# Another order of the column-group products, and two more load buffers beside the scatters, in an S5 + attention + expert block

## The chip, the cores and the metric

The kernel runs on one core of a Trainium2 chip. The core has a tensor engine (PE, which loads its weights as PEld), a vector engine (DVE), a scalar engine (ACT), GpSimd (POOL) and a sync engine (SP) that here issues nearly all loads. Sixteen DMA engines move data between HBM and the on-chip memory. The metric is the device time of one execution in microseconds (us); less is better.

## What is computed

One block over 256 tokens of width 2048, in fp32: a state-space mixer (S5) and a sparse attention side by side, a gated sum into the stream, and then a layer of 16384 experts of which each token uses 128. Cut to what the change touches:

```python
cond = jax.nn.silu(c) @ w_ada[l] + b_ada[l]                      # six vectors of 2048
sh1, sc1, g1, sh2, sc2, g2 = [m[:, None, :] for m in jnp.split(cond, N_ADA, axis=-1)]
...
y = (jnp.einsum('ghp,blgp->blgh', c_re, sr) - jnp.einsum('ghp,blgp->blgh', c_im, si)
     + d_skip * uf)                                              # S5's output from its states
...
x = x + g2 * peer(h2, w_q, k1, k2, exp_u, exp_v)
...
# peer: top 16 of 256 candidates in each of 8 heads -> expert ids ec, gates gc
a = jax.nn.gelu(jnp.einsum('cd,chkd->chk', xc, exp_u[ec]))
return jnp.einsum('chk,chkd->cd', gc * a, exp_v[ec])
```

## The kernel before

**Arithmetic.** A product of two fp32 matrices is made of three products of rounded halves. split() makes them from a loaded unit of 128 x 1024: ACT casts to hi (L99), DVE subtracts to lo (L102). lin_block() (L521) then runs hi*hi, hi*lo and lo*hi.

**Loads.** unit() (L91) lets SP issue a load of 512 KB into a ring called raw, of four buffers. SP's queue is in order: a load that waits for its buffer holds those behind it. w_ada goes through rings of its own, in the later stages through adap alone, with three buffers.

**Order.** The Tile framework's scheduler, with its own simulation of the times, sets the order of the instructions on each engine. What the program writes in a loop may therefore be taken apart and stand elsewhere on the engine, as early as its operands are expected.

**cond_job() (L440)** multiplies silu(c) by w_ada. A step takes two loads, which hold four tiles of 512 columns: tiles[0] and [1] are of the first load, [2] and [3] of the second. Four products follow (L449), each into 32 rows of one PSUM tile, so each uses another group of 32 columns of PE. There are 80 such steps of four, called quads here, spread over the first 620 us beside the other work.

**g2_job() (L1314)** does the same with one row of output for g2: two loads of w_g2 through raw, four products (L1318), 16 steps. It runs beside the g groups and the expert tiles from 884 to 1310 us. g2_end() (L1322) adds b_row to the four rows and stores them.

**s5_py() (L691)** takes the four results p, q, a2, c2 that DVE makes in that order (L683 to L686), and adds their products with CP into one PSUM tile (L710), in the order of the list quad["pq", n] (L687).

**u_tile() (L1151)** handles 128 experts of exp_u: two loads, two splits, 48 products into pa, and a gelu (L1165), which is multiplied into SA or SB. There are 128 of them, from 620 to 1573 us.

**Scatters.** look() finds the tokens of each expert tile, and places() (L1355 to L1396, scratch in a pool st) turns this into a place for each row, by products psx and a chain on DVE. After places(0, ...) the pool st is closed, and a pool gq takes memory there; before the change it holds the small tile of g2_end alone. The loop at L1428 runs one u_tile and four scatters (L1414, POOL's indirect DMAs from SA to wc) in turn, 88 scatters in all. Behind it, from 1573 to the end, the rows of exp_v are gathered and multiplied.

## Time and profile before

| | us |
|---|---|
| median of three runs | 1891.27 |
| the runs | 1888.39 to 1891.78 |
| the profiled execution | 1887.95 |
| its span | 1886.1 |
| PE busy in it | 1781.8 |
| DVE busy | 1381.6 |
| ACT busy | 804.6 |
| POOL busy | 824.4 |

The stages, in us from the start of the span: to 49 start and first parts of w_ada; to 188 the first input products and more of w_ada; to 377 S5 steps beside w_in; to 620 attention, its output and w_out; to 884 the queries and the top-k of the experts, beside expert tiles; to 1310 the g groups beside expert tiles and w_g2; to 1400 expert tiles and places(); to 1573 scatters beside the last expert tiles; to 1886 the rows of exp_v.

The profile is of one execution. A line of a timeline gives the start, the length, the engine, the line of the program, and what the instruction writes and reads; idle time before it stands in brackets with what ended it. A product L449 or L1318 of fp32 operands is two instructions in the trace, so four instructions there are two products here. Lengths of products overlap; the distance from one start to the next is what a product holds PE for.

### The profile page before, as it was taken

How to read it: one execution, taken by the hardware profiler on the slowest of the kernel's cores; microseconds unless marked ns; L12 is line 12 of the kernel's file. 1: busy time of each engine (PE TensorE's matmuls, PEld its weight loads, DVE VectorE, ACT ScalarE, POOL GpSimd, SP SyncE). 2: the span in 40 equal slices, each digit the busy share in tenths (PEclk: the TensorE clock that was granted, in tenths of full speed). 3: DMA queues.
4: the chain of work that ended last, by engine and by line, in shares of the span. 5: the costliest groups of instructions: out<-in, count | busy, mean ns of one | idle time of the engine just before them, and what ended most of it. 6: DMA issues, size and time to landing. Idle time of an engine off the chain costs nothing. (4 is left out here: it accounts for less than half of the span.)

```text
span 1886.1 us, 32604 instructions
## 1 busy us (share of the span) xinstructions
PE 1781.8 (94%) x12048; PEld 1488.0 (79%) x12048; DVE 1381.6 (73%) x2765; ACT 804.6 (43%) x1329; POOL 824.4 (44%) x926
## 2 busy tenths in 40 slices
PE   5999999999999899999999999999998999999895
PEld 2756655568666899999999898898998898777674
DVE  3636998756745698888999898998783457776666
ACT  3422211148634544444444444444432336555554
POOL 5923432201110210112787666665027665887532
PEclk9998999999999999999999999999998999999998
DMA  9987556785686455555565556556567779999972
GB/s 358 407 286 265 192 185 226 260 314 199 238 268 208 166 180 179 171 178 167 184 194 193 190 183 196 184 178 201 182 186 218 227 233 356 323 326 323 373 258 109
DMA packets 117839, 436.77 MB, mean 232 GB/s; under 512 B 17237, under 2 KB 19989, under 8 KB 107686
## 3 DMA queue, kind: packets, MB, share of 16 engines
q1 hardware_dynamic: 91440, 322.41, 51.3%
q0 software_dynamic: 22080, 108.62, 16.2%
q10 hardware_dynamic: 4150, 3.56, 0.6%
q8 instruction: 97, 1.59, 0.3%
q14 instruction: 72, 0.59, 0.1%
HBM read 411.38 MB, written 23.15 MB: 230 GB/s over the span
## 5 line engine op out<-in xcount | busy, mean ns | idle before, releaser
L102 DVE TENSOR_TENSOR lo<-raw,hi 128x1024 fp32r<-128x1024 f32 x382 | 512.9, 1345 | 229.6 <-ACT hi L99 188.3
L99 ACT CAST hi<-raw 128x1024 fp32r<-128x1024 f32 x385 | 402.1, 1047 | 590.7 <-PE pa L521 302.2
L521 PE MATMUL pa<-hhi,lo 128*128 128x256 f32 x2048 | 590.3, 288 | 10.1 <-DVE lo L102 6.7
L521 PE MATMUL pa<-hhi,hi 128*128 128x256 f32 x2048 | 583.6, 285 | 9.7 <-ACT hi L99 6.8
L521 PE MATMUL pa<-hlo,hi 128*128 128x256 f32 x2048 | 583.1, 285 | 0.0
L521 PEld LDWEIGHTS pa<-hhi,lo 128*128 128x128 f32 x2048 | 395.0, 193 | 38.3 <-DVE lo L102 11.1
L521 PEld LDWEIGHTS pa<-hhi,hi 128*128 128x128 f32 x2048 | 395.3, 193 | 10.8 <-ACT hi L99 8.0
L521 PEld LDWEIGHTS pa<-hlo,hi 128*128 128x128 f32 x2048 | 395.3, 193 | 0.5 <-issue 0.5
L1287 POOL TENSOR_TENSOR mv<-o,gp 128x256 fp32r<-128x256 f32 x256 | 186.4, 748 | 124.9 <-DVE o L1284 65.8
L1505 DVE TENSOR_TENSOR lv<-rv,hv 128x1024 fp32r<-128x1024 f32 x144 | 173.1, 1229 | 55.7 <-ACT hv L1504 52.3
L1504 ACT CAST hv<-rv 128x1024 fp32r<-128x1024 f32 x144 | 146.3, 1049 | 63.6 <-DMA rv<-in_peer_v,wt 40.7
L1284 DVE TENSOR_TENSOR o<-pT,iota 128x256 fp32r<-128x256 f32 (+1 forms) x256 | 124.8, 502 | 30.8 <-PE pgs L1290 17.9
L449 PE MATMUL cps<-adap,scz 128*32 128x512 f32 x476 | 113.8, 622 | 16.4 <-DMA adap<-in_w_ada 16.4
L1205 POOL TENSOR_TENSOR eq<-eq,iff 128x512 f32<-128x512 f32 x16 | 30.0, 1896 | 212.1 <-DVE eq L1204 212.1
L1305 POOL TENSOR_TENSOR SA<-SA,gs 128x50 f32<-128x50 f32 (+42 forms) x128 | 113.8, 904 | 12.9 <-ACT SA L1162 12.5
L1414 POOL DMA_INDIRECT wc<-SA,slot x88 | 97.1, 1103 | 46.1 <-issue 25.2
L1459 POOL DMA_INDIRECT rv<-in_peer_v,wt x74 | 97.3, 1316 | 45.2 <-DVE lv L1505 17.5
L521 PE MATMUL lin<-hhi,hi 128*128 128x256 f32 x352 | 104.8, 298 | 2.2 <-ACT sg L998 1.3
L521 PE MATMUL lin<-hlo,hi 128*128 128x256 f32 x352 | 102.9, 292 | 1.5 <-POOL hlo L1111 1.0
L521 PE MATMUL lin<-hhi,lo 128*128 128x256 f32 x352 | 102.6, 292 | 0.0
L1295 ACT COPY gs<-pgs 128x256 f32<-128x256 f32 x128 | 47.6, 373 | 121.7 <-POOL SA L1305 107.5
L521 PEld LDWEIGHTS lin<-hhi,hi 128*128 128x128 f32 x352 | 68.1, 194 | 26.3 <-issue 16.9
(450 smaller groups left out, 3291.9 us busy)
## 6 DMA issues: line engine op xcount, KB each, us to landing
raw<-in_peer_u SPq DMA_DIRECT2D x256, 512.0 KB
adap<-in_w_ada SPq DMA_DIRECT2D x119, 512.0 KB
raw<-in_w_in SPq DMA_DIRECT2D x32, 512.0 KB
raw<-in_w_out SPq DMA_DIRECT2D x32, 512.0 KB
raw<-in_peer_wq SPq DMA_DIRECT2D x32, 512.0 KB
raw<-in_w_g SPq DMA_DIRECT2D x32, 512.0 KB
raw<-in_w_inq SPq DMA_DIRECT2D x16, 512.0 KB
raw<-in_cmp_w SPq DMA_DIRECT2D x16, 512.0 KB
```

The source lines that it names most:

```text
L99: i = nc.scalar.copy(hi[:, :n], raw[:, :n])
L102: (lo_engine or nc.vector).tensor_tensor(out=lo[:, :n], in0=raw[:, :n], in1=hi[:, :n].bitcast(F32), op=OP.subtract)
L449: nc.tensor.matmul(ps[32 * g:32 * g + 32, :], scz[:, kt + g], tiles[g], start=kt == 0, stop=kt == KT - 4)
L521: nc.tensor.matmul(ps, w, a[:, kk], start=first and u == 0 and k == 0 and i == 0, stop=last and u == n - 1 and k == 7 and i == 2)
L1284: nc.vector.tensor_tensor(out=o, in0=bc(pT[:, j, t:t + 2].unsqueeze(2), shp), in1=io, op=OP.is_equal)
L1287: nc.gpsimd.tensor_tensor(out=mv[:, :, j], in0=o2, in1=g, op=OP.mult)
L1295: nc.scalar.copy(tmp, pv[:, 1])
L1305: nc.gpsimd.tensor_tensor(out=o, in0=o, in1=tmp[:, a0:m], op=OP.mult)
L1414: d = nc.gpsimd.indirect_dma_start(out=wcs[i], out_offset=bass.IndirectOffsetOnAxis(ap=ap, axis=0), in_=SB[:, m - NSA] if i else SA[:, m], ...
L1459: d = nc.gpsimd.indirect_dma_start(out=raw, out_offset=None, in_=A["peer_v"], in_offset=bass.IndirectOffsetOnAxis(ap=wt[:, 128:129].bitcas ...
L1504: nc.scalar.copy(hi, raw)
L1505: state["last"] = nc.vector.tensor_tensor(out=lo, in0=raw, in1=hi.bitcast(F32), op=OP.subtract).ins
```

## The change

Three things are altered. The loops over the column groups in cond_job and g2_job run 2, 3, 0, 1 and not 0 to 3, and the list of s5_py's operands begins with c2, which DVE makes last. g2_end puts its rows into a buffer of the ring raw. And gq now holds a ring rawx of two buffers, which u_tile uses for two of each six loads from the scatter loop to the end of the expert tiles: six buffers in all.

```diff
--- before.py
+++ after.py
@@ -445,7 +445,8 @@
             tiles = loaded[ran[0]]
             assert loads[ran[0]] == (j, q, kt // 2)
             ran[0] += 1
-            for g in range(4):
+
+            for g in (2, 3, 0, 1):
                 nc.tensor.matmul(ps[32 * g:32 * g + 32, :], scz[:, kt + g], tiles[g],
                                  start=kt == 0, stop=kt == KT - 4)
             if kt == KT - 4:
@@ -684,7 +685,7 @@
         v.tensor_tensor(out=q, in0=c, in1=ei, op=OP.mult)
         v.tensor_tensor(out=a2, in0=a, in1=ei, op=OP.mult)
         v.tensor_tensor(out=c2, in0=c, in1=er, op=OP.mult)
-        quad["pq", n] = (0, p), (2, q), (1, a2), (1, c2)
+        quad["pq", n] = (1, c2), (0, p), (2, q), (1, a2)
 
     zs = {"todo": [], "go": False}
 
@@ -1152,7 +1153,12 @@
         m = state["m"]
         if m >= NK:
             return
-        us = [split(unit(A["peer_u"][m, i]), keep=m == NK - 1) for i in range(2)]
+        us = []
+        for i in range(2):
+
+            more = state.get("more") and (2 * m + i) % 6 >= 4
+            r = unit(A["peer_u"][m, i], state["more"], "rawx", 2) if more else unit(A["peer_u"][m, i])
+            us.append(split(r, keep=m == NK - 1))
         ps = psA.tile([128, 512], F32, name="pa", tag="pa", bufs=2)
         lin_block(us, h2hi, h2lo, ps[:, :T])
         t = state["t"]
@@ -1314,13 +1320,13 @@
         for kt in range(KT):
             rs = [unit(A["w_g2"][kt * 128:(kt + 1) * 128, h * 1024:(h + 1) * 1024])
                   for h in range(2)]
-            for g in range(4):
+            for g in (2, 3, 0, 1):
                 nc.tensor.matmul(g2ps[32 * g:32 * g + 1, :], scol[:, kt:kt + 1],
                                  rs[g // 2][:, g % 2 * 512:(g % 2 + 1) * 512], start=kt == 0, stop=kt == KT - 1)
             yield
 
-    def g2_end(pool):
-        rows = pool.tile([128, 512], F32, name="g2r", tag="g2r")
+    def g2_end():
+        rows = buf("raw")[:, :512]
         for g in range(4):
             cs, r = slice(g * 512, (g + 1) * 512), slice(32 * g, 32 * g + 1)
             nc.gpsimd.dma_start(rows[r], A["b_row"][1:2, cs])
@@ -1427,7 +1433,8 @@
     sts.close()
     gqs = ExitStack()
     gq = gqs.enter_context(tc.tile_pool(name="gq", bufs=1))
-    g2_end(gq)
+    g2_end()
+    state["more"] = gq
     seen, sent = SORT, 0
     while sent < SORT:
         u_tile()
@@ -1478,6 +1485,7 @@
         if state["m"] >= seen + 8:
             look(seen, seen + 8)
             seen += 8
+    state["more"] = None
     gqs.close()
     psU.close()
```

On PE at the first row of w_g2 in the stage of the g groups (L1318 psg before; pa are expert tiles, pgs the g groups). Before:

```order
4158 L521 MATMUL pa<-hhi,lo 128x256
4159 L521 MATMUL pa<-hhi,hi 128x256
4160 L521 MATMUL pa<-hlo,hi 128x256
4161 L1318 MATMUL psg<-raw,scol 1x512 x2
4162 L521 MATMUL pa<-hhi,lo 128x256
...
4183 L1290 MATMUL pgs<-mv,o_8841 128x256 x2
4184 L521 MATMUL pa<-hhi,lo 128x256
4185 L521 MATMUL pa<-hhi,hi 128x256
4186 L521 MATMUL pa<-hlo,hi 128x256
4187 L1318 MATMUL psg<-raw,scol 1x512 x2
4188 L521 MATMUL pa<-hhi,lo 128x256
```

After the change, where the lines have moved down by six (L1318 is L1324, L521 is L522):

```order
4155 L522 MATMUL pa<-hhi,lo 128x256
4156 L522 MATMUL pa<-hhi,hi 128x256
4157 L522 MATMUL pa<-hlo,hi 128x256
4158 L1296 MATMUL pgs<-mv,o_8841 128x256 x2
4159 L1324 MATMUL psg<-raw,scol 1x512 x4
4160 L522 MATMUL pa<-hhi,lo 128x256
4161 L522 MATMUL pa<-hhi,hi 128x256
4162 L522 MATMUL pa<-hlo,hi 128x256
```

The two pairs, 26 rows apart before, are one run of four at the second one's place. The same holds for all 16 rows.

On PE near the end of w_out's products (L1013, lin), with the w_ada products of cond_job between them (L449, cps). Before:

```order
1979 L1013 MATMUL lin<-hi,mlo 128x512 x2
1980 L449 MATMUL cps<-adap,scz 32x512 x2
1981 L1013 MATMUL lin<-hi,mhi 128x512 x2
1982 L1013 MATMUL lin<-lo,mhi 128x512 x2
1983 L1013 MATMUL lin<-hi,mlo 128x512 x2
1984 L1013 MATMUL lin<-hi,mhi 128x512 x2
1985 L1013 MATMUL lin<-lo,mhi 128x512 x2
1986 L1013 MATMUL lin<-hi,mlo 128x512 x2
1987 L449 MATMUL cps<-adap,scz 32x512 x2
1988 L1013 MATMUL lin<-hi,mhi 128x512 x2
```

After (L1014 and L450):

```order
1994 L1014 MATMUL lin<-lo,mhi 128x512 x2
1995 L1014 MATMUL lin<-hi,mlo 128x512 x2
1996 L1014 MATMUL lin<-hi,mhi 128x512 x2
1997 L450 MATMUL cps<-adap,scz 32x512 x4
1998 L1014 MATMUL lin<-lo,mhi 128x512 x2
1999 L1014 MATMUL lin<-hi,mlo 128x512 x2
2000 L1014 MATMUL lin<-hi,mhi 128x512 x2
2001 L1014 MATMUL lin<-lo,mhi 128x512 x2
```

Two pairs with six rows between them are one run of four. Over the program L449 stood in 111 runs and L450 stands in 81: 6 and 5 in the first 49 us, 33 and 27 to 188 us, 34 and 24 to 377, 38 and 25 to 620. The runs of s5_py's products go from 41 to 29.

On DVE at the end of places() (place, the e's and w's are of it; slot is made for the scatters; lo are splits of expert tiles, mx is look()). Before:

```order
1964 L1380 TENSOR_REDUCE w<-X 128x88
1965 L1388 TENSOR_TENSOR w<-w 128x88
1966 L1394 TENSOR_REDUCE e<-e 128x1
1967 L102 TENSOR_TENSOR lo<-raw,hi 128x1024
1968 L1167 TENSOR_TENSOR SB<-SB,ga 128x2x128
1969 L1389 TENSOR_TENSOR w<-w 128x88
1970 L1396 COPY few<-e 128x1
1971 L1390 TENSOR_TENSOR place<-w 128x88
1972 L1406 CAST slot<-place 128x4
1973 L1350 TENSOR_REDUCE mx<-SB 128x16
1974 L1406 CAST slot<-place 128x4
1975 L102 TENSOR_TENSOR lo<-raw,hi 128x1024
```

After:

```order
1968 L1386 TENSOR_REDUCE w<-X 128x88
1969 L1394 TENSOR_TENSOR w<-w 128x88
1970 L1400 TENSOR_REDUCE e<-e 128x1
1971 L1395 TENSOR_TENSOR w<-w 128x88
1972 L1402 COPY few<-e 128x1
1973 L1396 TENSOR_TENSOR place<-w 128x88
1974 L1412 CAST slot<-place 128x4
1975 L1356 TENSOR_REDUCE mx<-SB 128x16
1976 L102 TENSOR_TENSOR lo<-rawx,hi 128x1024 x2
1977 L102 TENSOR_TENSOR lo<-raw,hi 128x1024 x2
1978 L1173 TENSOR_TENSOR SB<-SB,ga 128x2x128
```

Before, splits of expert tiles stand between the operations of places(). Now none stands from the start of places() to its end, and the next splits read rawx: their loads write memory that the scratch of places() held. In SP's queue the two loads into rawx stand behind the loads of the next tiles into raw.

## Rows read from the trace of the kernel before

**Rows 1.** The page's first part: busy us (share of the span) x instructions, by engine.

```profile
PE 1781.8 (94%) x12048; PEld 1488.0 (79%) x12048; DVE 1381.6 (73%) x2765; ACT 804.6 (43%) x1329; POOL 824.4 (44%) x926
```

**Rows 2.** Busy time by stage: us from:to, length, each engine (x instructions), PEclk, DMA share, GB/s.

```profile
49.00:146.00 97.00, 91.30 (x613) 60.96 (x613) 44.95 (x48) 29.32 (x38) 54.85 (x46) 1.00 0.93 347
188.00:283.00 95.00, 89.75 (x610) 57.57 (x609) 87.81 (x178) 22.98 (x33) 39.45 (x41) 0.98 0.54 187
283.00:377.00 94.00, 92.53 (x601) 54.38 (x601) 75.23 (x178) 15.06 (x27) 23.70 (x29) 0.97 0.70 243
377.00:620.00 243.00, 234.66 (x1251) 167.20 (x1249) 141.10 (x308) 127.65 (x256) 23.03 (x27) 0.99 0.72 248
884.00:1110.00 226.00, 224.87 (x1780) 206.56 (x1780) 206.72 (x460) 102.70 (x230) 164.32 (x217) 1.00 0.59 191
1110.00:1310.00 200.00, 195.43 (x1521) 177.93 (x1518) 180.96 (x388) 87.20 (x171) 129.28 (x165) 1.00 0.60 188
1400.00:1573.00 173.00, 156.53 (x1202) 152.04 (x1202) 83.39 (x110) 60.06 (x78) 109.55 (x108) 0.95 0.77 236
```

**Rows 3.** Timeline of PE, 376 to 415: start, us, line, operation [idle before <-releaser].

```profile
382.37 1.05 PE L449 MATMUL cps<-adap,scz 128*32 128x512 f32 x4 [0.51 <-DMA adap<-in_w_ada]
383.35 0.30 PE L786 MATMUL lin<-hhi,lo 128*24 128x256 f32 x1
...
412.51 1.06 PE L449 MATMUL cps<-adap,scz 128*32 128x512 f32 x8
413.51 0.72 PE L775 MATMUL lin<-lo,hhi 128*128 128x512 f32 x2
```

**Rows 4.** Timeline of PE at 203 us: a run of two products of L710.

```profile
203.06 0.63 PE L710 MATMUL py<-s,CP 128*32 128x256 f32 x4
203.62 0.39 PE L521 MATMUL lin<-hhi,lo 128*128 128x256 f32 x1
```

**Rows 5.** Timeline of PE at 888 us: a pair of L1318 between products of L521.

```profile
888.39 0.28 PE L521 MATMUL pa<-hlo,hi 128*128 128x256 f32 x1
888.60 1.03 PE L1318 MATMUL psg<-raw,scol 128*1 128x512 f32 x4
889.55 0.39 PE L521 MATMUL pa<-hhi,lo 128*128 128x256 f32 x1
889.78 0.28 PE L521 MATMUL pa<-hhi,hi 128*128 128x256 f32 x1
```

**Rows 6.** Timeline of PE from 1304 us: both pairs of one row of w_g2.

```profile
1304.10 1.03 PE L1318 MATMUL psg<-raw,scol 128*1 128x512 f32 x4 [0.68 <-DMA raw<-in_w_g]
...
1308.12 1.03 PE L1318 MATMUL psg<-raw,scol 128*1 128x512 f32 x4
```

**Rows 7.** Waits of PE from 884 to 1310: total us, times, longest.

```profile
PE psg L1318 <- DMA raw<-in_w_g: 4.2, 6, 1.2
```

**Rows 8.** Timeline of SP's queue at 1300 us: issues of loads.

```profile
1300.26 1.61 SPq L91 DMA_DIRECT2D raw<-in_w_g  x2
```

**Rows 9.** The gelu behind each expert tile (L1165): from 1322 to 1392, then 1388 to 1575.

```profile
L1165 ACT ACTIVATE ga<-pa x12: 373/377/380, 1327.2 to 1391.6; 128x256 f32<-128x256 f32 x12
...
L1165 ACT ACTIVATE ga<-pa x27: 374/377/381, 1391.6 to 1571.8; 128x256 f32<-128x256 f32 x27
```

**Rows 10.** Timelines of SP's queue and of ACT about the stall at 1445 us.

```profile
1433.82 0.33 SPq L91 DMA_DIRECT2D raw<-in_peer_u  x1
...
1452.10 1.04 ACT L99 CAST hi<-raw 128x1024 fp32r<-128x1024 f32 x1 [8.27 <-remote]
```

**Rows 11.** Waits of ACT from 1400 to 1573: total us, times, longest.

```profile
ACT hi L99 <- remote: 22.6, 5, 8.3
```

**Rows 12.** Timeline of DVE: first and last of a piece of places().

```profile
1395.96 0.69 DVE L1374 TENSOR_TENSOR_SCAN C<-tri,psx 128x264 f32<-128x264 f32 x1
...
1398.86 0.15 DVE L1394 TENSOR_REDUCE e<-e 128x1 f32<-128x3 f32 x1
```

**Rows 13.** Waits of SP's queue over the whole span: total us, times, longest.

```profile
SPq L91 <- PE cps L449: 161.5, 70, 10.0
```

## The prediction

> **What bounds the kernel now.** I read the shares of busy time first: the tensor engine is busy for 94% of the span, the next engine (DVE) for 73% [rows 1]. So time is won by giving PE less to do, or by closing its last gaps, and only where no second engine stands close behind. The table by stage says where that is [rows 2]. From 49 to 146 us the DMA share is 0.93. In the S5 stage (188 to 377) PE is busy for 94% and 98% of the two halves, but DVE for 92% and 80%. From 377 to 620 PE is at 97% with DVE at 58%: the one stage that is PE's alone. In the stage of the g groups (884 to 1310) PE is at 99% and 98%, DVE at 91% and 90%. From 1400 to 1573, where the scatters run, PE is busy for only 156.5 of 173 us, its clock is 0.95 and the DMA share 0.77. The margin to see: PE first nearly everywhere, DVE one step behind in the two longest stages.
>
> **Part 1, the order of the column groups.** The reader should see what a pair of column groups costs beside four. At 382.37 a pair of L449 stands alone, and the next product starts 0.98 us later; at 412.51 all four stand together, and the next starts 1.00 us later [rows 3]. Four cost what two cost, so each pair that joins its other half saves one whole visit: 0.98 us, and the two changes of shape about it. Those are seen at L1318: 0.21 us from the product before into the pair where the pace is 0.12, and 0.23 us after the first product behind it [rows 5], some 0.2 us in all. A visit is worth 0.98 to 1.18 us; I take 1.1.
>
> How many visits go is read from the order of PE's instructions. The program waits for the first load with groups 0 and 1 and for the second with 2 and 3, so the scheduler let it run as pairs. With group 2 first, the first product waits for the last load, and all four become ready together. L449 stands in 111 runs before, in 81 now: 6 fewer from the 49 us mark to 188, 10 fewer in the S5 stage, 13 fewer from 377 to 620. Before 49 us the loads bound the time; I take nothing there.
> - 49 to 188 us: 6 x 1.1 = 6.6 us of PE, but with a DMA share of 0.93 the loads end the stage. I take 1 us, bounds -3 (the loads now come in another order) and +4.
> - S5: 10 x 1.1 = 11 us. The new order in the quad of s5_py makes its first product wait for the last vector result c2, and L710's runs go from 41 to 29. A run of two such products holds PE for 0.56 us [rows 4]; what joining saves lies between the 0.2 us of the changes and that 0.56, so 12 runs give 2.4 to 6.7 us, and I take 3. Of these 14 us DVE can't follow all: it has 7.2 us free in the first 95 us and 18.8 in the next 94 [rows 2]. I take 7, bounds 2 and 14.
> - 377 to 620: 13 x 1.1 = 14.3 us, nothing else near. I take 12, bounds 7 and 15.
>
> **w_g2 in the g groups.** 32 pairs of L1318 become 16 fours. The pair at 888.60 held PE for 0.95 us, and 1.15 with both changes [rows 5]: 16 x 1.15 = 18.4 us. The first pair of a row also waits for its load, 0.68 us at 1304.10; the second, 4 us behind, doesn't [rows 6], and over the stage that wait is 4.2 us [rows 7]. The fours stand where the second pair stood, so it should go: 22.6 us at most. Against it: the first load's buffer is now held 4 us longer, and the load behind it on SP's queue comes later by as much. A load takes 3.84 us from its issue at 1300.26 [rows 8] to the start at 1304.10 [rows 6]; 64 expert tiles and 16 rows of w_g2 are 160 loads in 426 us, 2.7 us each, so a buffer comes round in 10.7; less the load, a cast of 1.04 [rows 10] and a subtraction of about that length, some 4.7 us are left, and the ring just bears it. And DVE has 19 us left in each half [rows 2]. I take the early half in full (10) and under half of the late one (5), so 15 us; bounds 8 and 21.
>
> **Part 2, six buffers while scatters run.** The gelu behind each expert tile counts the pace. Before the scatters, 11 periods take 64.4 us, 5.85 us each; from 1391.6 to 1571.8 there are 26, in 180.2 us [rows 9]. At 5.85 they would take 152, so 28 us are lost. The rows of the worst stall show how: SP issues a load at 1433.82, and the cast that needs it starts at 1452.10, after 8.27 us of waiting for it [rows 10]. With four buffers a buffer comes round in two tiles, 11.7 us, less cast and subtraction, some 2.1, that is 9.6 us of patience; with six it is 17.6 - 2.1 = 15.5. That load took 18.2 us, so six buffers leave about 3 us of this stall and of the shorter ones little. ACT's waits of this kind add up to 22.6 us [rows 11]. I give back 23 of the 28 us.
>
> What is new is a price at the start. The two extra buffers lie in memory that places() has just used, and the first tile that takes them is m=101. SP's load for it therefore waits until the whole chain of places has run, and PE has m=100 and the two products psx, and then nothing. Before, that chain ran between the splits of later tiles. Its length is in the trace: from C at 1395.96 to the end of the e at 1398.86 is 3.05 us, a dozen DVE operations [rows 12], and three short ones behind them, an estimate of 0.2 each after the last of those rows, make 3.7. Then the load, 3.84, and its cast, 1.04 [rows 10]: 8.6 us, with 1 to 2 us before psx, so about 10 us with no product, and some 1.5 us at the lower clock behind it. I put the stall at 11.5 us, bounds 8.5 and 14. The cover that hid it, the next tiles, is what was taken away. The part is worth 23 - 11.5 = 11.5 us; I take 11, bounds -4 (the buffers give back 8 only) and +18.
>
> The trace speaks of one load's landing time only, not of what held it. The Trainium skill, "DMA: Bandwidth & Descriptors", section "Queues, rings and completion order", says that each DMA engine takes turns between the queues it has work for, packet by packet. By that rule two more loads would stand in the same rings behind the same scatters and come no sooner than the loads before them. The mean share of 0.77 speaks against a full pipe; by the rule alone the part would be worth -11.5 and the forecast 22 us higher. That result is a rival below, priced there from rows.
>
> The remaining edit, rows of b_row taken from the ring of raw, moves four small stores ahead of the first scatter and takes one ring buffer for some microseconds a few tiles before places(); PE's cover there is the other three buffers. Nothing, at worst 2 us if that cover is gone.
>
> **Sum.** 1 + 7 + 12 + 15 + 11 = 46 us. The profiled execution took 1887.95 us, 1.85 us over its span of 1886.1, so 1842. The median of the three runs, 1891.27, is 3.3 us above that execution, so I forecast 1845 us.
>
> **Rivals.**
> - *The second engine takes it (about 1867).* DVE in the S5 stage and the late g groups, DMA before them, and part of the scatters: 0 + 2 + 10 + 8 + 4 = 24 us. For it: DVE at 92%, 91%, 90% [rows 2]. Against: these are shares below the full, and PE's own idle there is smaller still.
> - *All of it (about 1823).* 3 + 13 + 15 + 20 + 17 = 68 us. It needs DVE near 97% in the late g groups and the stall at its lower bound.
> - *The buffers hide nothing (about 1868).* The loads are late because the engines are shared, so six wait as four did: 35 - 11.5 = 23 us. The one load of 18.2 us speaks for it, the share of 0.77 against.
> - *Held loads (slower, about 1910).* The ring adap has three buffers. A quad that waits for both loads frees both only when it runs, so the second load of the next quad can't start before; SP's queue, which already waits 161.5 us in 70 places for cps to free a buffer [rows 13], holds everything behind it. From 188 to 620 us there are 44 quads, 9.8 us apart, against a load of 3.84 us. Where they stand closer than a load takes, each makes PE wait: at 1 us each 44 are lost. In the g groups the hold of 4 us uses up the ring's 4.7, and loads 2 us longer than 3.84 lose 1.3 x 16 = 21 where 15 were won. The sum is then 1 + 19 - 44 + 15 - 21 + 11 = -19, so 1910. It decides from 25 / 44 = 0.6 us a quad; the mean distance of 9.8 speaks against it.
> - *It does nothing (about 1891).* The runs are joined in the order, but the four don't run side by side because their loads end apart. The quad at 412.51 speaks against it.
>
> **How the numbers follow.** The forecast, with its terms within their middle, 0.48; the second engine 0.16; the buffers hiding nothing 0.12; all of it 0.12; held loads 0.08; nothing 0.04. The range of eight in ten reaches from all of it to just past the second engine and the idle buffers: 1824 to 1874. A measurement of this kernel can tell about 0.2% (4 us) from no change. Faster by more than that 0.88, within it 0.04, slower 0.08.
>
> **What would show it.** In the profile after: L449 and L1318 on PE in groups of eight instructions about 1.0 us apart from their neighbours; PE's waits for w_g2 gone; a distance between gelus of 26 tiles near 169 us instead of 180; one PE gap of about 10 us near 1355 to 1375, released by the cast of m=101, with the clock low behind it; DVE's share in the S5 stage and g groups up by 3 to 6 points. I am wrong in the S5 and g terms if these stages keep their length while PE's idle time, released by DVE, grows; wrong in the scatters if ACT's waits for loads stay near 22 us; and wrong in sign if PE waits for adap at most quads.

## The result, and the profile after

The changed kernel takes 1870.59 us in the median of six runs (1863.35 to 1876.09), the kernel before 1887.09 beside it: a ratio of 0.9914, 95% interval 0.9885 to 0.9942. Two repeats on other chips give 0.9870 (0.9849 to 0.9892) and 0.9892 (0.9867 to 0.9917). The forecast was 1845 us, 46 less than the median then shown; what came is 16.5 us in the first pair and 22 to 25 on the other chips. The sign is right, the size a third to a half of the forecast, and the time is within the range.

The page of the changed kernel, busy us by engine; its span is 1865.4 us:

```profile
PE 1737.6 (93%) x12048; PEld 1484.7 (80%) x12048; DVE 1399.1 (75%) x2765; ACT 799.3 (43%) x1325; POOL 820.3 (44%) x926
```

PE has 44 us less to do than in [rows 1], yet the span is only 20.7 us shorter: half of what was taken off PE became waiting. The same stages as in [rows 2], in the changed kernel (length, busy time of PE, PEld, DVE, ACT, POOL, then PEclk, DMA share, GB/s):

```profile
49.00:146.00 97.00, 90.02 (x608) 63.22 (x608) 47.92 (x48) 28.57 (x37) 53.89 (x46) 0.96 0.90 334
188.00:283.00 95.00, 91.60 (x677) 63.74 (x672) 90.50 (x185) 24.95 (x36) 32.37 (x38) 0.96 0.59 200
283.00:377.00 94.00, 88.72 (x588) 52.22 (x588) 78.83 (x180) 14.97 (x26) 25.76 (x30) 0.96 0.71 249
377.00:620.00 243.00, 231.95 (x1350) 177.10 (x1348) 150.86 (x322) 132.13 (x275) 30.06 (x39) 0.99 0.73 251
884.00:1110.00 226.00, 221.03 (x1806) 209.99 (x1805) 215.92 (x468) 104.80 (x234) 171.54 (x219) 1.00 0.59 192
1110.00:1310.00 200.00, 198.53 (x1604) 188.03 (x1604) 185.95 (x376) 90.99 (x170) 120.85 (x154) 1.00 0.60 198
1400.00:1573.00 173.00, 158.93 (x1192) 151.34 (x1191) 90.42 (x124) 68.96 (x91) 109.17 (x101) 0.97 0.80 251
```

DVE's share is up where it stood second (90.5 of 95 us in the S5 stage's first half, 215.9 of 226 in the early g groups), and PE's busy share in the second half of S5 fell from 98% to 94%, at a granted clock of 0.96 for 0.97. Since the stages move, the two traces are better laid beside each other by milestones of the program, the start of the first or the end of the last instruction of a kind, or the start of a single one. The first pair is the two profiled executions of this page, the second a pair from one other chip:

| milestone (us) | before | changed | won so far | before, other chip | changed, other chip | won so far |
|---|---|---|---|---|---|---|
| first product of w_in | 126.0 | 137.1 | -11.1 | 128.3 | 139.5 | -11.2 |
| end of the S5 input stage (L743's last) | 373.4 | 374.0 | -0.6 | 376.1 | 376.1 | 0.0 |
| first product of an expert tile | 632.8 | 618.6 | 14.2 | 637.3 | 620.8 | 16.5 |
| last product of the g groups | 1300.0 | 1274.7 | 25.3 | 1306.0 | 1276.5 | 29.5 |
| products psx of places() | 1393.9 | 1365.4 | 28.5 | 1399.9 | 1367.5 | 32.4 |
| gelu of expert tile 101 | 1398.4 | 1385.1 | 13.3 | 1404.4 | 1387.2 | 17.2 |
| gelu of expert tile 126 | 1571.8 | 1550.9 | 20.9 | 1551.2 | 1532.4 | 18.8 |
| last product of an expert tile | 1576.4 | 1555.6 | 20.8 | 1555.6 | 1537.1 | 18.5 |
| first product with exp_v | 1576.8 | 1556.0 | 20.8 | 1566.0 | 1537.5 | 28.5 |
| end of the span | 1886.1 | 1865.4 | 20.7 | 1877.0 | 1849.4 | 27.6 |

So nothing is won up to 377 us, 14.8 to 16.5 us from there to the expert tiles, and 11 to 13 in the g groups. The products psx come another 3 us earlier, but that is a matter of their place in PE's order: from the last g product to them are 90.7 to 91.0 us in the changed kernel and 92.0 to 94.1 in all kernels with four buffers. From psx to the last expert tile 8 to 14 us are lost, those 3 among them. Counted from the last g product, 12.0 and 12.3 us are lost up to tile 101; from there to tile 126, 7.6 us come back in the first pair and 1.6 in the second. The gelus from tile 101 to tile 126, first to last start, in the order of the table:

```profile
L1165 ACT ACTIVATE ga<-pa x26: 374/378/381, 1398.4 to 1571.8; 128x256 f32<-128x256 f32 x26
L1171 ACT ACTIVATE ga<-pa x26: 374/379/381, 1385.1 to 1550.9; 128x256 f32<-128x256 f32 x26
L1165 ACT ACTIVATE ga<-pa x26: 376/380/381, 1404.4 to 1551.2; 128x256 f32<-128x256 f32 x26
L1171 ACT ACTIVATE ga<-pa x26: 375/380/381, 1387.2 to 1532.4; 128x256 f32<-128x256 f32 x26
```

PE's timeline in the changed kernel shows the fours (start, length, line, tiles, count; L450 is w_ada, L1324 w_g2):

```profile
391.89 1.06 PE L450 MATMUL cps<-adap,scz 128*32 128x512 f32 x8
392.89 0.50 PE L776 MATMUL lin<-hi,hhi 128*128 128x512 f32 x1
...
402.71 1.06 PE L450 MATMUL cps<-adap,scz 128*32 128x512 f32 x8
403.70 0.50 PE L776 MATMUL lin<-lo,hhi 128*128 128x512 f32 x1
...
873.40 1.04 PE L1324 MATMUL psg<-raw,scol 128*1 128x512 f32 x8
874.37 0.39 PE L522 MATMUL pa<-hhi,lo 128*128 128x256 f32 x1
```

Eight instructions, that is four products, hold PE for 1.00, 0.99 and 0.97 us, as the four in [rows 3] did and hardly more than the pairs in [rows 3, 5], 0.98 and 0.95. Waits of PE in the g groups (from 870 to 1290 us; total, times, longest):

```profile
PE psg L1324 <- DMA raw<-in_w_g: 1.4, 2, 1.2
```

The waits for w_g2 went from 4.2 us in [rows 7] to 1.4. Waits of PE from 49 to 377 us:

```profile
PE py L711 <- DVE s L687: 10.4, 3, 5.2
```

That line is new in size: 10.4 us of waiting for the vector results of S5, 2.9 us before. It is where visits saved in that stage went.

The loss is at expert tile 101. PE's timeline there, then SP's and ACT's:

```profile
1365.41 1.05 PE L1378 MATMUL psx<-f,tri 128*128 128x264 f32 x4
1375.15 0.58 PE L522 MATMUL pa<-hhi,hi 128*128 128x256 f32 x1 [8.68 <-ACT hi L99]
```

```profile
1370.21 8.00 SPq L91 DMA_DIRECT2D rawx<-in_peer_u  x4
```

```profile
1374.05 1.04 ACT L99 CAST hi<-rawx 128x1024 fp32r<-128x1024 f32 x1 [8.06 <-DMA rawx<-in_peer_u]
```

The two products psx end PE's queue at 1365.4; SP issues the load of tile 101, the first of the four in its row, at 1370.21, as soon as the chain of places() has left its memory; the cast starts 3.84 us later at 1374.05, having waited 8.06 us, and the next product at 1375.15 after 8.68 us of nothing. From one gelu to the next are 19.4 us there, 13.6 over the pace of 5.8, and 12.0 net by the table. That is the stall that the prediction put at 11.5 us, bounds 8.5 and 14. Behind it ACT waits for loads (from 1365 to 1560 us; "remote" stands where no instruction of the core is seen to end the wait, here the landing of a load):

```profile
ACT hi L99 <- remote: 24.8, 5, 8.0
ACT hi L99 <- DMA rawx<-in_peer_u: 8.5, 2, 8.1
```

The waits of the first kind stand at 24.8 us with six buffers, 22.6 with four in [rows 11]. By them nothing was given back; by the gelus above, 7.6 us were, of the 23 forecast.

### The profile page after: what moved, and what is told of

It is laid out like the page before. It is cut to its first block, busy times and chain, and to the rows that moved or that the text cites. A ratio compares the mean times of both kernels' runs of the same rounds, so it can differ in the third digit from the quotient of the medians.

```text
span 1865.4 us, 32601 instructions
## 1 busy us (share of the span) xinstructions
PE 1737.6 (93%) x12048; PEld 1484.7 (80%) x12048; DVE 1399.1 (75%) x2765; ACT 799.3 (43%) x1325; POOL 820.3 (44%) x926
## 5 line engine op out<-in xcount | busy, mean ns | idle before, releaser
L102 DVE TENSOR_TENSOR lo<-raw,hi 128x1024 fp32r<-128x1024 f32 x364 | 494.2, 1359 | 196.2 <-ACT hi L99 159.8
L99 ACT CAST hi<-raw 128x1024 fp32r<-128x1024 f32 (+1 forms) x367 | 383.3, 1047 | 512.5 <-PE pa L522 245.1
L522 PE MATMUL pa<-hhi,lo 128*128 128x256 f32 x2048 | 590.3, 288 | 13.0 <-DVE lo L102 10.1
L522 PE MATMUL pa<-hhi,hi 128*128 128x256 f32 x2048 | 582.7, 285 | 14.9 <-ACT hi L99 13.2
L522 PE MATMUL pa<-hlo,hi 128*128 128x256 f32 x2048 | 582.3, 284 | 1.4 <-issue 1.2
L522 PEld LDWEIGHTS pa<-hhi,lo 128*128 128x128 f32 x2048 | 394.2, 192 | 35.8 <-DVE lo L102 15.5
L522 PEld LDWEIGHTS pa<-hhi,hi 128*128 128x128 f32 x2048 | 394.7, 193 | 15.6 <-ACT hi L99 14.6
L522 PEld LDWEIGHTS pa<-hlo,hi 128*128 128x128 f32 x2048 | 394.7, 193 | 2.3 <-issue 2.3
L1293 POOL TENSOR_TENSOR mv<-o,gp 128x256 fp32r<-128x256 f32 x256 | 180.0, 723 | 110.4 <-DVE o L1290 72.1
L1290 DVE TENSOR_TENSOR o<-pT,iota 128x256 f32<-128x256 f32 (+1 forms) x256 | 132.2, 542 | 13.4 <-POOL mv L1293 9.8
L1311 POOL TENSOR_TENSOR SA<-SA,gs 128x50 f32<-128x50 f32 (+42 forms) x128 | 123.8, 982 | 10.7 <-ACT SA L1168 10.6
L522 PE MATMUL lin<-hhi,hi 128*128 128x256 f32 x352 | 104.4, 297 | 5.1 <-ACT sg L999 2.3
L522 PE MATMUL lin<-hlo,hi 128*128 128x256 f32 x352 | 102.6, 292 | 1.3 <-POOL hlo L1112 1.3
L522 PE MATMUL lin<-hhi,lo 128*128 128x256 f32 x352 | 101.8, 289 | 1.0 <-DVE lo L102 1.0
L450 PE MATMUL cps<-adap,scz 128*32 128x512 f32 x476 | 87.0, 621 | 1.3 <-DMA adap<-in_w_ada 1.3
L522 PEld LDWEIGHTS lin<-hhi,hi 128*128 128x128 f32 x352 | 68.4, 195 | 20.9 <-issue 13.6
```

Source lines behind the costliest of these rows:

```text
L99: i = nc.scalar.copy(hi[:, :n], raw[:, :n])
L102: (lo_engine or nc.vector).tensor_tensor(out=lo[:, :n], in0=raw[:, :n], in1=hi[:, :n].bitcast(F32), op=OP.subtract)
L450: nc.tensor.matmul(ps[32 * g:32 * g + 32, :], scz[:, kt + g], tiles[g], start=kt == 0, stop=kt == KT - 4)
L522: nc.tensor.matmul(ps, w, a[:, kk], start=first and u == 0 and k == 0 and i == 0, stop=last and u == n - 1 and k == 7 and i == 2)
L1290: nc.vector.tensor_tensor(out=o, in0=bc(pT[:, j, t:t + 2].unsqueeze(2), shp), in1=io, op=OP.is_equal)
L1293: nc.gpsimd.tensor_tensor(out=mv[:, :, j], in0=o2, in1=g, op=OP.mult)
```

## The experiments

All were timed beside the kernel before on the same chip, and their ratios are to that. Chips differ: the kernel before takes 1885 and 1891 us on two of them, 1872.3 to 1872.7 on three others.

**The parts alone, on one chip.** Four kernels, each with one part. First the order in cond_job:

```diff
-            for g in range(4):
+            for g in (2, 3, 0, 1):
                 nc.tensor.matmul(ps[32 * g:32 * g + 32, :], scz[:, kt + g], tiles[g],
```

> The kernel before with one edit: cond_job runs its column groups 2, 3, 0, 1. Theory: it holds all that the trace after shows of this edit: some 14 us won from 377 to 620 us, some 7 in the S5 stage, and the 8 us lost before 180 us, because the first product of a quad now waits for the later load while the loads of w_ada end that stage. Total -13 us, ratio 0.993, with the first product of w_in (L521, 126.0 us before) near 135. Rival: the early loss comes from another part (the scheduler's new order through s5_py); then the first product of w_in stays near 126 and the ratio is 0.989.

Measured: 1882.57 us, ratio 0.9989 (0.9973 to 1.0005). Its trace has the first product of w_in at 139.3, so the early delay is this edit's, and S5's end at 376.7; the expert tiles begin 9.6 us earlier than in the trace before. One trace and the medians don't agree: 8 us won at psx in the trace, which is among the fastest of its twelve executions, and 2 (-1 to 5) by the ratio. What this edit gives alone isn't settled beyond that. PE's waits for S5's vector results are 9.7 us in this trace.

The same order in g2_job:

```diff
-            for g in range(4):
+            for g in (2, 3, 0, 1):
                 nc.tensor.matmul(g2ps[32 * g:32 * g + 1, :], scol[:, kt:kt + 1],
```

> The kernel before with one edit: g2_job runs its column groups 2, 3, 0, 1. Theory: the g stage is PE-bound enough to give 12 to 13 us (what the two traces differ by between the first and the last of its products), nothing elsewhere: ratio 0.993, PE's waits of 4.2 us for w_g2 gone. Rival: DVE takes the late half, 5 to 8 us, ratio 0.9965.

Measured: 1867.71 us, ratio 0.9918 (0.9895 to 0.9941), 15 us by the ratio; in the trace 12.6 us are won up to psx, 9.5 of them in the g groups. Their products before and with this edit, first to last start:

```profile
L1290 PE MATMUL pgs<-mv,o x256: 274/279/387, 887.9 to 1299.7; 128*128 128x256 f32 x128
L1290 PE MATMUL pgs<-mv,o x256: 274/279/387, 886.7 to 1289.0; 128*128 128x256 f32 x128
```

The first half of these products takes 192.1 us for 194.2, the second 210.5 for 217.9. DVE didn't take the late half; it took most of the early one. PE's waits for w_g2 are 2.8 us here, not gone. In all the traces the g groups take 411 to 415 us with the old order (six traces) and 401 to 403 with the new (fourteen).

The list in s5_py:

```diff
-        quad["pq", n] = (0, p), (2, q), (1, a2), (1, c2)
+        quad["pq", n] = (1, c2), (0, p), (2, q), (1, a2)
```

> The kernel before with one edit: the list of s5_py's operands begins with c2. Theory: PE's waits for DVE's s in front of L710, 2.9 us before and 10 us in the trace after, come from this edit, since PE's queue now stands at c2, the last of four; it wins 3 us of joined runs and loses 3 to 7: ratio 1.000 to 1.002. Rival: the joined runs win and the waits came with the other order of w_ada: -3 us, ratio 0.9985.

Measured: 1883.95 us, ratio 0.9995 (0.9983 to 1.0008): nothing. Its trace has 3.4 us of PE's waits for S5's vector results, where the order in cond_job alone has 9.7: the rival is right that these waits came with the order of w_ada.

The two buffers, with all three orders as before:

```diff
     gq = gqs.enter_context(tc.tile_pool(name="gq", bufs=1))
-    g2_end(gq)
+    g2_end()
+    state["more"] = gq
```

> The changed kernel with the three orders put back, so that only the two rawx buffers (and the rows of b_row in the ring raw) are new. Theory: the stall at expert tile 101 is there, 13 to 14 us between two gelus over the pace, and the buffers give back 8 to 9 of the 29 us that the scatter stage loses: +5 us, ratio 1.003. Rival: in the order of this kernel the stall is hidden, or the buffers give back most: -10 us, ratio 0.995.

Measured: 1889.80 us, ratio 1.0021 (1.0005 to 1.0036), with 18.8 us between two gelus at tile 101: slower, as the theory had it. From the gelu of tile 101 to that of 126 are 161.3 us here, 168.5 to 171.7 in the three other traces of this chip, all with four buffers: some 9 us come back behind the stall, the theory's 8 to 9. The four parts add up to -0.8%, the changed kernel had -0.9%: by these numbers they don't hide each other.

**Parts put back, on a second chip.** The changed kernel with four buffers:

```diff
-    state["more"] = gq
```

> The changed kernel without the two rawx buffers (four buffers stay; the rows of b_row stay in the ring raw). Theory: the buffers cost 4 to 5 us net (the kernel with them alone was 1.0021 of before), so without them the change gives 16.5 + 4 = 20 us, ratio 0.989; the stage from the products psx to the last expert tile is 182 us as before (190 in the changed kernel) and no PE gap of 8.7 us stands before tile 101. Rival: the stall is not the buffers' but of the products coming earlier; then the ratio stays at 0.9914.

Measured: 1865.67 us, ratio 0.9848 (0.9825 to 0.9872), less than the theory's 0.989, which was reckoned from another chip; the changed kernel did not run on this one. The buffers from tile 104 on, which need no memory of places() in a hurry:

```diff
-    state["more"] = gq
     seen, sent = SORT, 0
     while sent < SORT:
         u_tile()
+        if state["m"] >= 103:
+            state["more"] = gq
```

> The changed kernel with the rawx buffers taken from expert tile 104 on instead of 101, so that no load waits for the memory of places(). Theory: the stall of 13.6 us at tile 101 goes and the 8 to 9 us that the buffers give back stay: 13 us less than the changed kernel, ratio 0.9845. Rival: the loads are late because the scatters hold the DMA engines, the buffers give back nothing by themselves, and what they seemed to give was the scatters' later start: then it equals the kernel with four buffers, 0.989.

Measured: 1865.29 us, ratio 0.9847 (0.9816 to 0.9877). The stall is gone in both. ACT's waits for loads from 1380 to 1550 us, with four buffers and then with six:

```profile
ACT hi L99 <- remote: 36.8, 6, 10.1
```

```profile
ACT hi L99 <- remote: 21.5, 4, 8.6
```

The six take 15 us off ACT's waits, but from psx to the last expert tile are 184.9 and 181.7 us, and the times are equal within their intervals, which leave room for some 7 us either way. The ratio is the theory's, the equality with four buffers is the rival's; by one trace each the six give back 3 us. From tile 101 to 126 are 175.4 and 172.2 us, 169.6 in the mix below, also six from tile 104, and 163.4 in the next kernel, which takes them from 101 with the stall. So part of what comes back behind a stall may be the stall's own doing, since the scatters start later; that isn't settled.

The old order in the first 32 quads:

```diff
-            for g in (2, 3, 0, 1):
+            for g in (2, 3, 0, 1) if ran[0] > 32 else range(4):
```

> The changed kernel with the old order of the column groups (0 to 3) in the first 32 quads of cond_job, those of the first 150 us, and the new one in the other 48. Theory: the 8 to 10 us lost before 150 us come from those 32 quads, whose loads are held in their buffers until the later one lands while the loads end that stage (DMA at 409 GB/s before and 353 in the changed kernel, 49 to 92 us). So the first product of w_in is back at 126 to 128 us, and 7 to 10 us are won on the changed kernel: ratio 0.987. Rival: what is won there is taken back in the S5 stage, where DVE is second: ratio 0.991.

Measured: 1869.93 us, ratio 0.9871 (0.985 to 0.9893). That is the theory's ratio, but it can't be read against the changed kernel on another chip. On this one it stands 4 us behind the kernel with four buffers (0.9848), and in its trace the two buffers don't cost that: from the last g product to the last expert tile are 278.0 us, 278.5 with four. The first product of w_in is back at 128.6, yet S5's input products (L631) begin at 168.7, where 164.3 to 169.2 stand in every trace, and the stage ends at 377.2: what was won early is taken back there, as the rival says. The row of 49 to 92 us shows the early delay, in the kernel before, the changed one and this one:

```profile
49.00:92.00 43.00, 41.50 (x313) 32.40 (x314) 26.17 (x21) 18.06 (x24) 41.35 (x32) 1.00 1.03 409
```

```profile
49.00:92.00 43.00, 38.17 (x275) 29.23 (x275) 23.91 (x19) 16.77 (x24) 41.28 (x34) 0.96 0.93 353
```

```profile
49.00:92.00 43.00, 40.34 (x299) 32.08 (x300) 28.43 (x21) 17.62 (x23) 41.35 (x32) 0.96 0.99 384
```

Loads came at 409 GB/s before, at 353 with the fours from the start, at 384 with the fours from quad 33 on. The ten traces with the fours from the start have 337 to 354, the ten others 384 to 409. That a load held until its partner lands keeps its buffer, and so stops SP's queue, is my reading and isn't shown: in this stretch SP waits 11.7 us for the w_ada products before and 11.1 in the changed kernel, and what grows is its wait for the splits of other loads, from 2.8 to 7.6 us.

All these together, without the edit in s5_py:

> A mix: the old order in the first 32 quads, the new one in the other 48 and in g2_job, the old list in s5_py, and the rawx buffers from tile 104 on. Theory: the sum of the parts: 17 us of w_g2, 10 of the later quads, 5 to 9 of the buffers: 32 to 36 us, ratio 0.982. Rival: buffers give nothing and the S5 stage takes back the early gain: ratio 0.988.

Measured: 1864.75 us, ratio 0.9864 (0.984 to 0.9887): 0.982 did not come, and it is no better than the simple removal of the buffers.

**Are the late loads held by rows of scatters?** In most of the traces so far the casts that waited longest began 1 to 2 us behind the end of a row of scatters that POOL had issued back to back (1450.1 + 1.0 and 1452.1 in the kernel before). I formed the theory that a load lands only when POOL pauses, and put a product of its own on POOL behind every fourth scatter:

```diff
+    pz = gq.tile([128, 512], F32, name="pz", tag="pz")
+    nc.gpsimd.memset(pz, 0.0)
     while sent < SORT:
         u_tile()
         for _ in range(PACE):
-            scatter(sent)
+            scatter(sent, state.get("gap"))
             sent += 1
+            if sent % 4 == 0:
+                with tc.issue_after(state["sc"]):
+                    state["gap"] = nc.gpsimd.tensor_tensor(out=pz, in0=pz, in1=pz, op=OP.mult).ins
```

On a third chip, first the changed kernel again:

> The changed kernel once more, beside the next three on one chip. It should repeat 0.9914 of before (its interval was 0.9885 to 0.9942), with 185 to 190 us from the products psx to the last expert tile and one distance of 19 us between two gelus at tile 101.

Measured: 1847.99 us, ratio 0.9870 (0.9849 to 0.9892). From psx to the last expert tile are 169.7 us, not 190, with the one distance of 19.7 at tile 101 and no other above 7.4. With the pauses and four buffers:

> The changed kernel without the rawx buffers, and with one product of 128 x 512 on POOL (about 1.9 us) after every fourth scatter, so that POOL can't issue more than four scatters in a row. Its result isn't used. Theory: a load of an expert tile that is out while POOL issues scatters back to back lands 1 to 2 us after the last of them (in five traces the casts that waited longest began 1.1 to 1.9 us behind the end of a row of 8 to 20 scatters), so no row is longer than four now, a load lands in each pause, and the stage from psx to the last expert tile falls from 181 us to 165 to 170, with no distance between gelus above 8: 12 to 16 us less than with four buffers (0.9848 on another chip), ratio 0.978. Rival: the loads wait for the volume that the scatters move, and the rows of scatters end because the tiles stop, not the other way round; then pauses change nothing (0.985), or the later scatters delay the end.

Measured: 1862.35 us, ratio 0.9945 (0.9927 to 0.9962), slower than without. POOL's timeline, and what PE waited for from 1530 to 1570:

```profile
1388.13 1.16 POOL L1420 DMA_INDIRECT wc<-SA,slot  x1 [0.30 <-issue]
1389.32 1.05 POOL L1448 TENSOR_TENSOR pz<-pz 128x512 f32<-128x512 f32 x1
1390.53 1.01 POOL L1420 DMA_INDIRECT wc<-SA,slot  x1 [0.17 <-issue]
```

```profile
PE accv L1542 <- ACT ga L1171: 16.0, 1, 16.0
```

The pauses are there (1.05 us each), the last scatters come later, and PE waits 16.0 us between the expert tiles and exp_v. Before the change with pauses alone, and the mix with them:

> The kernel before with only the pauses of POOL after every fourth scatter. Theory: 12 to 16 us faster than before, ratio 0.993, all of it between psx and the last expert tile (182 us before, 167 to 170 then). Rival: no change, ratio 1.000.

Measured: 1886.74 us, ratio 1.0087 (1.0063 to 1.011).

> A mix: w_g2's new order, the new order in the last 48 quads of cond_job and the old one in the first 32, the old list in s5_py, four buffers, and the pauses of POOL. Theory: 17 us of w_g2, 9 of the later quads, 12 to 16 of the pauses: 38 to 42 us, ratio 0.979. Rival: the pauses give nothing: ratio 0.986.

Measured: 1858.61 us, ratio 0.9935 (0.9917 to 0.9954). On this chip the pauses had nothing to win: the changed kernel issues 84 scatters in one row from 1387 to 1509 us, and no cast waits for a load in it. A chip with late loads never ran them, but its traces answer the theory. In that of cond_job's order alone, POOL issues 36 scatters back to back from 1416.2 to 1467.7 us, and the cast that waited longest starts in the middle of them:

```profile
1459.51 1.04 ACT L99 CAST hi<-raw 128x1024 fp32r<-128x1024 f32 x1 [9.65 <-remote]
1458.66 0.97 POOL L1414 DMA_INDIRECT wc<-SA,slot  x1 [0.30 <-issue]
1459.93 0.97 POOL L1414 DMA_INDIRECT wc<-SA,slot  x1 [0.30 <-issue]
```

The traces of w_g2's order and of the list in s5_py have such a cast too. So the theory falls. The rows end because the tiles stop: behind the row that ends at 1456.7 in the changed kernel, POOL waits for the places of the next scatters, which DVE makes behind the next tile:

```profile
1461.95 0.97 POOL L1420 DMA_INDIRECT wc<-SA,slot  x1 [5.25 <-DVE slot L1412]
```

**Chip or kernel?** So the kernel before, the changed one and the two with the stall removed ran on one more chip, the second pair of the table above:

> The kernel before, for a trace on the same chip as the next three. Theory: whether loads come late beside the scatters depends on the chip, not on the kernel. On a chip with late loads this trace has 180 to 185 us between psx and the last expert tile and 20 us of ACT's waits for loads; on one without, 163 to 166 us and none. Ratio 1.000. Rival: it depends on the kernel (on how many scatters stand in a row), and this trace has 180 to 185 us on any chip.

> The changed kernel on the same chip. Theory: the stall of 13 to 14 us at tile 101 on any chip. With late loads 187 us from psx to the last expert tile and a ratio of 0.991, without them 170 us and 0.987.

> The changed kernel without the two rawx buffers, on the same chip. Theory: the buffers give back nothing on either kind of chip and cost the stall, so this is 5 to 13 us faster than the changed kernel: ratio 0.984 to 0.985 with late loads, 0.980 without, and from psx to the last expert tile what the kernel before has on this chip. Rival: on a chip without late loads the stall at tile 101 is taken up behind it, since the next stage waits for the last scatter and not for the last tile: ratio 0.987 as the changed kernel.

> The changed kernel with the rawx buffers from tile 104 on, on the same chip. Theory: no stall at tile 101 and nothing given back: equal to the kernel with four buffers within 0.2%. Rival: with late loads six buffers do give back some of the waits: 5 us below the kernel with four.

Measured: 1872.62 us (ratio 1.0001, 0.9987 to 1.0016), 1850.70 (0.9892, 0.9867 to 0.9917), 1838.31 (0.9814, 0.9793 to 0.9834) and 1842.43 (0.9838, 0.982 to 0.9857). From psx to the last expert tile 155.7, 169.6, 155.6 and 155.6 us: the chip decides, not the kernel, though the theory had 163 to 166 for the first. Of the eighteen traces of the experiments, the ten on three chips have no late load and the eight on the other two all have them. Each chip was measured at one time only, so chip and time can't be told apart. The stretch of 1400 to 1510 us in the first three (columns as above):

```profile
1400.00:1510.00 110.00, 108.83 (x900) 108.10 (x899) 65.31 (x96) 44.51 (x56) 81.78 (x76) 1.00 0.88 255
```

```profile
1400.00:1510.00 110.00, 109.78 (x911) 109.18 (x910) 60.49 (x80) 45.20 (x57) 86.88 (x76) 1.00 0.94 271
```

```profile
1400.00:1510.00 110.00, 109.85 (x913) 109.45 (x913) 58.43 (x76) 45.20 (x57) 83.97 (x78) 1.00 0.92 271
```

PE is busy for 108.8 of 110 us in the kernel before, with four buffers, its clock whole, and the DMA share 0.88. The only waits of ACT for a split there (1400 to 1550 us) are for PE:

```profile
ACT hi L99 <- PE pa L521: 91.2, 52, 2.8
```

And the scatters of the changed kernel, 84 of them in one row:

```profile
L1420 POOL DMA_INDIRECT wc<-SA,slot x88: 965/972/1757, 1372.6 to 1510.0; - x88
```

There is nothing on this chip that six buffers could give back. The stall is all that is left of them: 13.9 us from psx on, 11.4 from the last g product to the last expert tile (260.6 us, 249.2 with four buffers), 12.4 by the medians. The kernel with the buffers from tile 104 on is 4 us slower than the one with four, 0.24% where the theory had 0.2%, with intervals that overlap.

**The S5 visits.** Last, on a fifth chip, the four buffers with the new order of cond_job only from quad 57 on, that is from 377 us:

```diff
-            for g in (2, 3, 0, 1):
+            for g in (2, 3, 0, 1) if ran[0] > 56 else range(4):
```

> The kernel with four buffers and all three orders, but with the new order of cond_job only in its last 24 quads, those from 377 us on; the first 56 run 0 to 3 as before. Theory: the visits saved before 377 us are worth nothing, since DVE's chain sets the S5 stage and the loads what stands before it, so this equals the kernel with all quads in the new order within 0.3% (0.981 to 0.985, by the chip). Rival: the ten visits saved in the S5 stage are worth the 7 us of the prediction: 0.4% slower than that kernel.

> The kernel with four buffers and all three orders, beside the one above on the same chip: 0.981 on a chip without late loads, 0.985 on one with.

Measured: 1845.09 us, ratio 0.985 (0.9823 to 0.9878), against 1840.78, 0.9827 (0.9799 to 0.9856). The 56 early quads are worth 4 us by the medians, with intervals that overlap: between nothing and what was forecast. Waits of PE from 150 to 377 us, without them and with them:

```profile
PE py L711 <- DVE s L687: 3.1, 2, 1.9
```

```profile
PE py L711 <- DVE s L687: 11.9, 3, 5.2
```

PE waits 9 us longer for S5's vector results when its visits before 377 us are fewer.

## Why the prediction was right or wrong

- **Four cost what two cost: right.** 0.97 to 1.00 us for a four [rows 3, 5].
- **377 to 620 us, 12 us: right by the traces.** 14.8 and 16.5 us in the two pairs, of which some 4 may be what the earlier quads left behind. Over all traces the expert tiles begin at 631 to 637 us with the old order of cond_job and at 618 to 628 with the new one in all quads, 12 us earlier on average. The time of that edit alone, 2 us (-1 to 5) better, doesn't show it, and that stays open.
- **w_g2, 15 us: right in sum, not in its halves.** 11.1 and 13.0 in the pairs, 12.6 up to psx in the trace of that edit alone, 15 by its ratio. But I took 10 for the early half, as PE's alone, and 5 for the late one: over all traces the early half gave 2, with DVE at 96% in the changed kernel, the late one 7 to 12.
- **49 to 188 us, +1 with bounds -3 and +4: wrong there, without a price.** The first product of w_in comes 11 us later. The failed step: I let another order of the loads cost 3 us at most and kept held loads for the slower rival alone, and the load rate fell by 14% while the loads end the stage. By which wait isn't shown. At the end it cost nothing: S5's chain begins at 164 to 169 us in all twenty traces.
- **S5, 7 us: too high, or not there.** I took half of the visits' worth because DVE had 7 and 19 us free. Free time on an engine isn't slack of a chain: from L631's first to L743's last the stage takes 204 to 210 us in all twenty traces, whatever PE has to do, and the saved visits came back as 10.4 us of waiting for s. By the last experiment this and the term before are worth 4 us together, not 8, and that isn't settled.
- **The scatter stage, +11 us: wrong by 19 to 25 from psx on, by 15 to 22 from the last g product on.** The stall was named, placed and priced: 12.0 and 12.3 us net for 11.5. The failed step is the 23 us on the other side, of which 7.6 and 1.6 came. First, the 28 us that [rows 9] show as lost belong to the chip on which that trace was taken: with the same kernel another chip loses none. Second, where loads are late, two more buffers took off 3 to 12 us of the 22 to 29 lost, by one trace each, and without the stall nothing that the time shows: 0.9847 beside 0.9848. I had one load's age (18.2 us) and made a patience of 15.5 us the answer to it; on the chips with late loads the longest from issue to cast is 17 to 27 us, trace by trace, with four buffers as with six. The rival "the buffers hide nothing", to which I gave 0.12 and 1868 us, has the number (1870.6) in part by luck: something was given back, and S5, which it counted in full, gave less.
- **The rule of the Trainium skill, "DMA: Bandwidth & Descriptors", "Queues, rings and completion order".** By it the part would have given nothing back; the pairs gave 7.6 and 1.6 us. That taking turns is the cause of the late loads isn't shown: on chips without late loads the same 84 scatters stand beside the same loads at a DMA share of 0.94, and none is late.
- **The rows of b_row, nothing: wrong where no load is late.** POOL's timeline in the kernel before on the second pair's chip:

```profile
1407.48 1.95 POOL L1326 DMA_DIRECT2D g2r<-in_b_row  x4 [81.91 <-DVE slot L1406]
...
1421.04 1.09 POOL L1328 DMA_DIRECT2D g2d<-g2r  x2
...
1428.38 1.08 POOL L1328 DMA_DIRECT2D g2d<-g2r  x2
```

The four loads of b_row and the stores take 4.1 us of POOL's time in front of the scatters and among them. Where tiles aren't late, the rows that exp_v needs are gathered behind the last scatter; ACT waits for them, with a gelu behind it in its order, and PE waits for that gelu. ACT before the change, then PE's wait before and with four buffers after it:

```profile
1560.99 1.99 ACT L1504 CAST hv<-rv 128x1024 fp32r<-128x1024 f32 x2 [9.40 <-DMA rv<-in_peer_v,wt]
```

```profile
PE accv L1529 <- ACT ga L1165: 10.4, 1, 10.4
```

```profile
PE accv L1536 <- ACT ga L1171: 2.9, 1, 2.9
```

The cover that made this edit worth nothing in the trace of before, the late tiles, was again that chip's. Between the two kernels 7.5 us of that wait are gone. That they are all this edit's isn't shown: no run has it alone.

Without the two buffers the forecast would have been the other terms' 35 us; that kernel is 34.0 us faster on one chip (0.9814), 31.9 on another and 25.5 on a chip with late loads. It beats the kernel before on all three, and the changed one by 12.4 us on the one chip where both ran.

## What to carry to other kernels

A buffer taken from memory that has just been let go isn't free: its first load waits for the last reader of that memory, and on a queue in order everything behind waits too; begin a few tiles later. Here that took the stall away; beside four buffers it gave no time that shows. Before a stall is priced as something to win back, see whether it is there on another chip: the stage that looked worst here was sound on three of the five chips of the experiments. And where the chain of another engine sets a stage's length, as in S5, work taken off PE comes back as waiting. The busy share alone doesn't tell where: with DVE at 91% in one half of the g groups and 90% in the other, 2 us came in the first and 7 to 12 in the second.

## What the runs showed of the hardware

Chips of one kind differed beside scatters. On three of them 88 scatters of POOL and the loads of the expert tiles ran together at DMA shares of 0.88 to 0.94 with no load late; on two others a load could stand up to 27 us between its issue and its cast, at mean shares of 0.76 to 0.82, and the same kernel took 12 to 19 us longer. What holds a load on those chips isn't settled. It is not the length of a row of scatters: there a late load was cast within a row of 36, and elsewhere rows of 84 and 88 held none. Two more buffers took off a part of the loss at most.
